# Trace of a batched product: A held whole per batch in two buffers, the next A loaded between the current B row tiles, B worked row tile by row tile, the last B tiles loaded in column pieces

## The chip, the cores and the metric

The kernel runs on one core of one Trainium2 chip. Times are device microseconds of that core. "Time" is the time of a whole execution, given as the median of several; "span" is the time from the first to the last instruction in the one profiled execution of a kernel, and it is about 1.7 us shorter than the time. All positions in time ("at 693.7 us") count from the start of the span.

## The reference, cut to what matters

```python
def setup_inputs():
    B, N = 8, 2176
    return {"a": randn(B, N, N) as float32, "b": randn(B, N, N) as float32}

def reference(a, b):
    prod = np.matmul(a, b)
    return np.diagonal(prod, axis1=1, axis2=2).sum(axis=-1)    # 8 numbers
```

The trace of A·B is the sum of A[i,k]·B[k,i] over all i and k. No matrix product is needed: each element of A meets one element of the transposed B once. The inputs are 303 MB, and every byte is used once.

## The kernel before

2176 is 17 blocks of 128. A and B arrive as row tiles of 128 x 2176 elements; the load casts them from float32 to bfloat16, so 544 KB are written for each (the page has 303.04 MB read and 151.54 MB written by the loads). TensorE transposes 128 x 128 blocks of B into PSUM (the memory of the kernel's `psum` tiles), and VectorE multiplies each such strip with the matching part of A and sums it into one column of `acc` (one custom product instruction, CUSTOM_DVE_ANT_0, and one short one that by its name reads the accumulator; the page has 680 of each, 602 and 82 ns in the mean). B is worked in groups of four row tiles: for each column block j, the four blocks of the group are transposed side by side, which gives products of 512 columns. The fifth group has one tile, and products of 128 columns.

```python
    KGW = 4                                            # B row tiles in a group
    a_pool = ctx.enter_context(tc.tile_pool(name="a_pool", bufs=2 * NT))     # 34 tiles, two batches
    b_pool = ctx.enter_context(tc.tile_pool(name="b_pool", bufs=2 * KGW))    # 8 tiles
    ...
    for bi in range(BATCH):
        for j_blk in range(NT):
            a_tile = a_pool.tile([P, N], dt, tag="a")
            nc.gpsimd.dma_start(out=a_tile, in_=a[bi, j_blk * P:(j_blk + 1) * P, :])
        for kg in range(N_KG):                         # 4, 4, 4, 4, 1 tiles
            for kc in range(kc_lo, kc_hi):
                b_tile = b_pool.tile([P, N], dt, tag="b")
                nc.gpsimd.dma_start(out=b_tile, in_=b[bi, kc * P:(kc + 1) * P, :])
            for j_blk in range(NT):
                psum_tile = psum_pool.tile([P, F], dt, tag="bT")
                for i, b_tile in enumerate(b_chunks):
                    nc.tensor.transpose(psum_tile[:, i * P:(i + 1) * P],
                                        b_tile[:, j_blk * P:(j_blk + 1) * P], identity)
                nc.vector.tensor_tensor_reduce(out=scratch[:, :fw],
                    in0=a_tiles[j_blk][:, kc_lo * P:kc_hi * P], in1=psum_tile[:, :fw],
                    ..., accum_out=acc[:, ...])
        # ... sum of acc into one column per batch
    # ... after the last batch: matmul with ones over the partitions, copy, store of 8 numbers
```

At most eight loads are in flight: in both traces no load issue starts before the load eight issues ahead of it has landed (0.28 us after it at the earliest, 0.53 us in the median). I take that for a limit of the framework that schedules the program.

Of the kernel before, what the change touches and what calls it, by code (L numbers as in the profile page):

```python
# [1 line left out]

# [6 lines left out]


@with_exitstack
def kernel(
    ctx: ExitStack,
    tc: tile.TileContext,
    a: bass.AP,
    b: bass.AP,
    out: bass.AP,
):
    nc = tc.nc  # L20
    P = 128
    BATCH, N, N2 = a.shape
    assert N == N2
    assert N % P == 0
    NT = N // P

    KGW = 4
    F = KGW * P
    N_KG = (NT + KGW - 1) // KGW

    dt = mybir.dt.bfloat16

    const = ctx.enter_context(tc.tile_pool(name="const", bufs=1))
    identity = const.tile([P, P], dt, tag="identity")
    make_identity(nc, identity)
    ones = const.tile([P, 1], mybir.dt.float32, tag="ones")
    nc.vector.memset(ones, 1.0)  # L37
    batch_accs = const.tile([P, BATCH], mybir.dt.float32, tag="batch_accs")
    result_tile = const.tile([P, BATCH], mybir.dt.float32, tag="result")

    a_pool = ctx.enter_context(tc.tile_pool(name="a_pool", bufs=2 * NT))
    b_pool = ctx.enter_context(tc.tile_pool(name="b_pool", bufs=2 * KGW))
    psum_pool = ctx.enter_context(tc.tile_pool(name="psum", bufs=7, space=bass.MemoryType.PSUM))
    psum_small = ctx.enter_context(tc.tile_pool(name="psum_small", bufs=1, space=bass.MemoryType.PSUM))
    scratch_pool = ctx.enter_context(tc.tile_pool(name="scratch", bufs=4))
    acc_pool = ctx.enter_context(tc.tile_pool(name="acc", bufs=2))

    for bi in range(BATCH):
        a_tiles = []
        for j_blk in range(NT):  # L50
            a_tile = a_pool.tile([P, N], dt, tag="a")
            nc.gpsimd.dma_start(out=a_tile, in_=a[bi, j_blk * P:(j_blk + 1) * P, :])  # L52
            a_tiles.append(a_tile)

        acc = acc_pool.tile([P, NT * N_KG], mybir.dt.float32, tag="acc")

        for kg in range(N_KG):
            kc_lo = kg * KGW
            kc_hi = min(kc_lo + KGW, NT)
            gw = kc_hi - kc_lo  # L60
            fw = gw * P

            b_chunks = []
            for kc in range(kc_lo, kc_hi):
                b_tile = b_pool.tile([P, N], dt, tag="b")
                nc.gpsimd.dma_start(out=b_tile, in_=b[bi, kc * P:(kc + 1) * P, :])  # L66
                b_chunks.append(b_tile)

            for j_blk in range(NT):
                psum_tile = psum_pool.tile([P, F], dt, tag="bT")  # L70
                for i, b_tile in enumerate(b_chunks):
                    nc.tensor.transpose(  # L72
                        psum_tile[:, i * P:(i + 1) * P],
                        b_tile[:, j_blk * P:(j_blk + 1) * P],
                        identity,
                    )
                scratch = scratch_pool.tile([P, F], dt, tag="scr")
                nc.vector.tensor_tensor_reduce(  # L78
                    out=scratch[:, :fw],
                    in0=a_tiles[j_blk][:, kc_lo * P:kc_hi * P],  # L80
                    in1=psum_tile[:, :fw],
                    scale=1.0,
                    scalar=0.0,
                    op0=mybir.AluOpType.mult,
                    op1=mybir.AluOpType.add,
                    accum_out=acc[:, j_blk * N_KG + kg: j_blk * N_KG + kg + 1],
                )

        nc.vector.reduce_sum(  # L89
            out=batch_accs[:, bi:bi + 1], in_=acc, axis=mybir.AxisListType.X  # L90
        )

    batch_psum = psum_small.tile([1, BATCH], mybir.dt.float32, tag="bp")
    nc.tensor.matmul(batch_psum, ones, batch_accs, start=True, stop=True)  # L94
    nc.vector.tensor_copy(out=result_tile[:1, :BATCH], in_=batch_psum)  # L95

    nc.sync.dma_start(
        out=out.rearrange("(a b) -> a b", a=1),
        in_=result_tile[:1, :BATCH],
    )  # L100


# [1 line left out]
_INS = ['a', 'b']  # L104
_OUTS = [((8,), 'float32')]


# [23 lines left out]
```

## Time and profile before

| | before |
|---|---|
| time, median of 3 | 737.29 us (737.23 to 737.42) |
| span | 735.6 us |
| full DMA rate | 213 to 215 GB/s written, twice that read |
| last load landed (landing records) | 721.2 us |
| last product to end of span | 2.7 us |

The lines below are from the page of the kernel before: the span, the busy time of each engine with its share, one row of the picture in 40 slices of 18.4 us (GB/s is what the core's 16 DMA engines wrote), and two of the DMA queues with packets, MB and their share of the 16 engines' span.

```profile
span 735.6 us, 7232 instructions
...
PE 271.7 (37%) x2314; PEld 217.7 (30%) x2314; DVE 364.8 (50%) x1370; POOL 144.4 (20%) x278
...
GB/s 175 213 214 215 213 215 213 214 214 214 214 213 214 214 214 214 213 214 213 214 214 213 214 213 214 214 213 215 213 214 214 213 214 214 214 214 213 161 209 29
...
q8 instruction: 18, 0.29, 0.1%
q14 instruction: 20, 0.16, 0.1%
```

No compute engine is near its limit: VectorE (DVE) is busy half the time. The GB/s row stands at 213 to 215 from the second slice to slice 37. Two slices stand out: 161 in slice 38, and 29 in the last. The two queues that the page marks "instruction" I read, by that name, as fetches of the program itself: 18 of 16 KB on q8 and 20 of 8 KB on q14 in the DMA records.

The next lines are stretches of time: busy time and count for each engine, the granted TensorE clock, the DMA share and GB/s.

```profile
core 0: us, PE busy (x) PEld busy (x) DVE busy (x) POOL busy (x), PEclk, DMA share, GB/s
...
690.00:697.00 7.00, 4.24 (x28) 2.74 (x26) 7.00 (x25) 2.11 (x4) 0.50 0.47 83
697.00:710.00 13.00, 8.40 (x86) 7.42 (x87) 12.30 (x41) 2.12 (x4) 0.76 1.05 212
710.00:715.00 5.00, 4.78 (x50) 4.58 (x48) 5.00 (x17) 0.00 (x0) 0.62 1.06 214
715.00:720.00 5.00, 1.94 (x19) 1.57 (x17) 4.94 (x17) 0.53 (x1) 0.72 0.95 178
```

Between 690 and 697 us the DMA writes 83 GB/s in place of 214. The timeline of GpSimd (POOL), which issues the loads, says why; the columns are start, duration, engine, line, operation, and in brackets how long the engine was idle before and what ended that.

```profile
676.64 0.53 POOL L66 DMA_DIRECT2D b_tile<-in_b_dram  x1 [2.12 <-DMA a_tile<-in_a_dram]
693.69 2.11 POOL L66 DMA_DIRECT2D b_tile<-in_b_dram  x4 [16.52 <-PE psum_tile L72]
704.09 2.12 POOL L66 DMA_DIRECT2D b_tile<-in_b_dram  x4 [8.29 <-PE psum_tile L72]
```

In the last batch no A loads are left to issue between the B loads, so GpSimd waits 16.52 us until TensorE has used up a group of B tiles and frees their buffers. After that comes the end of the kernel, here in the timeline of VectorE:

```profile
719.56 0.68 DVE L78 CUSTOM_DVE_ANT_0 scratch<-a_tile,psum_tile 128x512 bf16<-128x512 bf16 x1
...
720.17 0.68 DVE L78 CUSTOM_DVE_ANT_0 scratch<-a_tile,psum_tile 128x512 bf16<-128x512 bf16 x1
...
729.30 0.28 DVE L78 CUSTOM_DVE_ANT_0 scratch<-a_tile,psum_tile 128x128 bf16<-128x128 bf16 x1
...
729.51 0.28 DVE L78 CUSTOM_DVE_ANT_0 scratch<-a_tile,psum_tile 128x128 bf16<-128x128 bf16 x1
...
732.63 0.28 DVE L78 CUSTOM_DVE_ANT_0 scratch<-a_tile,psum_tile 128x128 bf16<-128x128 bf16 x1
...
732.96 0.24 DVE L89 TENSOR_REDUCE batch_accs<-acc 128x1 f32<-128x85 f32 x1
733.49 0.15 DVE L95 COPY result_tile<-batch_psum 1x8 f32<-1x8 f32 x1 [0.29 <-PE batch_psum L94]
```

Products of 512 columns follow each other every 0.61 us, those of 128 columns every 0.205 us. The last load has landed at 721.2 us, but VectorE has the rest of the fourth group and all of the fifth still before it, until 732.9 us; then come the sum of the batch, the matmul with ones, the copy and the store.

The trace also records 16 completions for each load (4354 in all: 16 for each of 272 loads, and 2), which I read as one for each of the core's 16 DMA engines. These records are not in a view of the profile; numbers called "landing records" in this text were worked out from them: the landing of a load is the last of its 16 completions, and its spread is the time from the first to the last. For the 11th load the spread is 0.78 us; for the 255th of 272 it is 7.38 us, and of these the last completion alone is 4.46 us behind the 15th. The records don't name the engine; I read the last completion as that of one engine that falls behind the others by more and more, called the slowest engine here. TensorE's first transpose of a B tile, where it waits for nothing else, starts 0.04 us after the last of the 16 completions.

### The profile page before, as it was taken

Reading aid. Unit: us, or ns where it says so; the run is one execution under the profiler, and the core shown is the slowest. Engines: PE = TensorE matmul, PEld = TensorE weight load, DVE = VectorE, ACT = ScalarE, POOL = GpSimd, SP = SyncE. Lnnn points to the kernel's source line nnn. Section 1 sums busy time; section 2 is a strip of 40 time slices with the busy share of each in tenths; the row PEclk is TensorE's granted clock in tenths of the full one; section 3 lists DMA queues with packets and bytes.
Section 4 is the critical chain, followed back from the end, with each engine's and each line's share of the span. In section 5 each row is a group of like instructions: output and inputs, shape, how many; then the busy total and the mean of one; then the engine's idle time right before and its main releaser. Section 6 shows DMA issues by size and latency. Waiting matters only on the chain.

```text
span 735.6 us, 7232 instructions
## 1 busy us (share of the span) xinstructions
PE 271.7 (37%) x2314; PEld 217.7 (30%) x2314; DVE 364.8 (50%) x1370; POOL 144.4 (20%) x278
## 2 busy tenths in 40 slices
PE   0016441174412744035450453505453054520665
PEld 0005430163301533024340343403342034410454
DVE  0007673087610967019570285704766056750698
POOL 4221221112121221212222122221222222221110
PEclk9999775557655556556655556555556556665575
DMA  8999999999999999999999999999999999999891
GB/s 175 213 214 215 213 215 213 214 214 214 214 213 214 214 214 214 213 214 213 214 214 213 214 213 214 214 213 215 213 214 214 213 214 214 214 214 213 161 209 29
DMA packets 39208, 152.00 MB, mean 207 GB/s; under 512 B 4354, under 2 KB 4354, under 8 KB 39170
## 3 DMA queue, kind: packets, MB, share of 16 engines
q0 software_dynamic: 39168, 151.54, 102.2%
q8 instruction: 18, 0.29, 0.1%
q14 instruction: 20, 0.16, 0.1%
q1 hardware_dynamic: 2, 0.00, 0.0%
HBM read 303.04 MB, written 0.00 MB: 412 GB/s over the span
## 4 chain that ended last, share of the span: by engine, by line
DMA 80%; issue 16%; POOL 1%; DVE 1%; PE 0%; POOLq 0%; DVEq 0%
DMA b_tile<-in_b_dram 51%; DMA a_tile<-in_a_dram 29%; POOL b_tile L66 1%; DVE scratch L78 1%; DVE acc L78 1%; POOL a_tile L52 0%; PE psum_tile L72 0%; POOLq L66 0%; POOL identity masks.py:199 0%; DVE batch_accs L89 0%; PE batch_psum L94 0%; DVEq L78 0%; POOL identity masks.py:197 0%; DVE result_tile L95 0%; POOLq masks.py:199 0%
## 5 line engine op out<-in xcount | busy, mean ns | idle before, releaser
L78 DVE CUSTOM_DVE_ANT_0 scratch<-a_tile,psum_tile 128x512 bf16<-128x512 bf16 (+1 forms) x680 | 362.3, 602 | 367.4 <-PE psum_tile L72 367.2
L72 PE MATMUL psum_tile<-identity,b_tile 128*128 128x128 bf16 x2312 | 271.5, 286 | 460.3 <-DMA b_tile<-in_b_dram 434.1
L72 PEld LDWEIGHTS <-b_tile 128*128 128x128 bf16 x2312 | 217.6, 132 | 513.8 <-DMA b_tile<-in_b_dram 465.6
L66 POOL DMA_DIRECT2D b_tile<-in_b_dram x136 | 71.8, 532 | 332.6 <-PE psum_tile L72 180.2
L52 POOL DMA_DIRECT2D a_tile<-in_a_dram x136 | 72.2, 533 | 238.0 <-DMA b_tile<-in_b_dram 112.4
L78 DVE DVE_READ_ACCUMULATOR2_ANT acc<- 128x1 f32 x680 | 55.9, 82 | 0.0
L89 DVE TENSOR_REDUCE batch_accs<-acc 128x1 f32<-128x85 f32 x8 | 1.9, 241 | 0.3
L94 PE MATMUL batch_psum<-batch_accs,ones 128*1 128x8 f32 x2 | 0.2, 173 | 1.5 <-DVE batch_accs L89 1.5
L94 PEld LDWEIGHTS batch_psum<-batch_accs,ones 128*1 128x1 f32 x2 | 0.1, 80 | 1.8 <-DVE batch_accs L89 1.8
L37 DVE MEMSET ones<- 128x1 f32 x1 | 0.1, 59 | 0.8 <-PEq L115 0.8
masks.py:199 POOL TENSOR_SCALAR_AFFINE_SELECT identity<-identity 128x128 bf16<-128x128 bf16 x1 | 0.3, 305 | 0.1
L95 DVE COPY result_tile<-batch_psum 1x8 f32<-1x8 f32 x1 | 0.2, 155 | 0.3 <-PE batch_psum L94 0.3
masks.py:197 POOL MEMSET identity<- 128x128 bf16 x1 | 0.2, 204 | 0.3 <-POOLq L115 0.3
L115 POOL MEMSET const-float32-0.0<- 128x1 f32 x1 | 0.1, 98 | 0.2 <-issue 0.2
L115 POOL MEMSET const-bfloat16-1.0<- 128x1 bf16 x1 | 0.1, 101 | 0.0
L115 POOL MEMSET const-uint8-127<- 128x1 uint8 x1 | 0.1, 101 | 0.0
L115 POOL MEMSET const-float32-1.0<- 128x1 f32 x1 | 0.1, 98 | 0.0
## 6 DMA issues: line engine op xcount, KB each, us to landing
a_tile<-in_a_dram POOLq DMA_DIRECT2D x136, 544.0 KB, 20.6
b_tile<-in_b_dram POOLq DMA_DIRECT2D x136, 544.0 KB, 20.3
out_dram<-result_tile SPq DMA_DIRECT2D x1, 0.0 KB
```

Of the source, the lines that this page charges most:

```text
L37: nc.vector.memset(ones, 1.0)
L52: nc.gpsimd.dma_start(out=a_tile, in_=a[bi, j_blk * P:(j_blk + 1) * P, :])
L66: nc.gpsimd.dma_start(out=b_tile, in_=b[bi, kc * P:(kc + 1) * P, :])
L72: nc.tensor.transpose(psum_tile[:, i * P:(i + 1) * P], b_tile[:, j_blk * P:(j_blk + 1) * P], identity,)
L78: nc.vector.tensor_tensor_reduce(out=scratch[:, :fw], in0=a_tiles[j_blk][:, kc_lo * P:kc_hi * P], in1=psum_tile[:, :fw], scale=1.0, scalar ...
L89: nc.vector.reduce_sum(out=batch_accs[:, bi:bi + 1], in_=acc, axis=mybir.AxisListType.X)
L94: nc.tensor.matmul(batch_psum, ones, batch_accs, start=True, stop=True)
L95: nc.vector.tensor_copy(out=result_tile[:1, :BATCH], in_=batch_psum)
L115: nc = _bacc.Bacc("TRN2", target_bir_lowering=False, num_devices=1)
```

## The change

Its intent: hold the whole A of a batch as one tile, so that one product can span several row tiles of A; then each B row tile can be worked off by itself as soon as it lands, with products of 768, 768 and 640 columns, and no group of four has to be complete first. The next A is loaded between the B tiles, so that GpSimd has something to issue. The last two B tiles come in four column pieces, so that work on them can start before they are complete.

```diff
-    a_pool = ctx.enter_context(tc.tile_pool(name="a_pool", bufs=2 * NT))
-    b_pool = ctx.enter_context(tc.tile_pool(name="b_pool", bufs=2 * KGW))
+    CHUNKS = [(0, 6), (6, 12), (12, NT)]
+    LAST_CHUNKS = [(0, 6), (6, 12), (12, 16), (16, NT)]
+    a_pool = ctx.enter_context(tc.tile_pool(name="a_pool", bufs=2))      # tiles [P, NT, N]
+    b_pool = ctx.enter_context(tc.tile_pool(name="b_pool", bufs=10))     # tiles [P, ROWS, N]
+    a_next = a_pool.tile([P, NT, N], dt, tag="a")
+    for gi in range(len(groups)):
+        load_a(a_next, 0, gi)                        # all 17 row tiles of the first A
     ...
+    for bi in range(BATCH):
+        a_all = a_next
+        last = bi == BATCH - 1
+        if not last:
+            a_next = a_pool.tile([P, NT, N], dt, tag="a")
+        for gi, (start, m) in enumerate(b_groups):   # ROWS = 1: m is 1, 17 tiles
+            b_tile = b_pool.tile([P, ROWS, N], dt, tag="b")
+            pieces = last and gi >= len(b_groups) - 2
+            chunks = LAST_CHUNKS if pieces else CHUNKS
+            if pieces:
+                for lo, hi in chunks:
+                    nc.gpsimd.dma_start(out=b_tile[:, 0, lo * P:hi * P],
+                                        in_=b[bi, start:start + P, lo * P:hi * P])
+            else:
+                load(b_tile[:, 0:m, :], b[bi], start, m)
+            if not last:
+                load_a(a_next, bi + 1, gi)
+            for lo, hi in chunks:
+                ...
+                psum_tile = psum_pool.tile([P, 6, P], dt, tag="bT")
+                for u in range(lo, hi):
+                    nc.tensor.transpose(psum_tile[:, u - lo, :], b_tile[...], identity)
+                nc.vector.tensor_tensor_reduce(out=scratch[:, :w, :],
+                    in0=a_all[:, lo:hi, start + s:...], in1=psum_tile[:, :w, :],
+                    ..., accum_out=acc[:, col:col + 1])
```

More of the change, by code (lines that the diff above doesn't have):

```diff
@@ L5, with row_groups @@
 import concourse.tile as tile
-from concourse import bass_utils, mybir
-from concourse import bass_isa
+from concourse import mybir
 from concourse.masks import make_identity
 from concourse._compat import with_exitstack
+def row_groups(n, p, rows):
+    groups, at = [], 0
+    while at < n:
+        m = min(rows, (n - at) // p)
+        groups.append((at, m))
+        at += m * p
+    return groups
 @with_exitstack
@@ L22 @@
     BATCH, N, N2 = a.shape
-    assert N == N2
-    assert N % P == 0
+    assert N == N2 and N % P == 0
     NT = N // P
-    KGW = 4
-    F = KGW * P
-    N_KG = (NT + KGW - 1) // KGW
+    ROWS = 1
+    CHUNKS = [(0, 6), (6, 12), (12, NT)]
+    LAST_CHUNKS = [(0, 6), (6, 12), (12, 16), (16, NT)]
     dt = mybir.dt.bfloat16
+    f32 = mybir.dt.float32
     const = ctx.enter_context(tc.tile_pool(name="const", bufs=1))
+    a_pool = ctx.enter_context(tc.tile_pool(name="a_pool", bufs=2))
+    b_pool = ctx.enter_context(tc.tile_pool(name="b_pool", bufs=10))
@@ new lines, with load @@
+    psum_pool = ctx.enter_context(tc.tile_pool(name="psum", bufs=7, space=bass.MemoryType.PSUM))
+    psum_small = ctx.enter_context(tc.tile_pool(name="psum_small", bufs=1, space=bass.MemoryType.PSUM))
+    scratch_pool = ctx.enter_context(tc.tile_pool(name="scratch", bufs=2))
+    acc_pool = ctx.enter_context(tc.tile_pool(name="acc", bufs=2))
+    groups = row_groups(N, P, ROWS)
+    slot_cols = [(start + r, m) for start, m in groups for r in range(m)]
+    def load(dst, src, start, m):
+        rows = src[start:start + P * m, :].rearrange("(p r) k -> p r k", r=m)
+        nc.gpsimd.dma_start(out=dst, in_=rows)
@@ L34, with load_a @@
+    def load_a(a_all, bi, gi):
+        start, m = groups[gi]
+        slot = start // P
+        load(a_all[:, slot:slot + m, :], a[bi], start, m)
+    a_next = a_pool.tile([P, NT, N], dt, tag="a")
+    for gi in range(len(groups)):
+        load_a(a_next, 0, gi)
     identity = const.tile([P, P], dt, tag="identity")
     make_identity(nc, identity)
-    ones = const.tile([P, 1], mybir.dt.float32, tag="ones")
+    ones = const.tile([P, 1], f32, tag="ones")
     nc.vector.memset(ones, 1.0)
-    batch_accs = const.tile([P, BATCH], mybir.dt.float32, tag="batch_accs")
@@ L39 @@
-    result_tile = const.tile([P, BATCH], mybir.dt.float32, tag="result")
-    a_pool = ctx.enter_context(tc.tile_pool(name="a_pool", bufs=2 * NT))
-    b_pool = ctx.enter_context(tc.tile_pool(name="b_pool", bufs=2 * KGW))
-    psum_pool = ctx.enter_context(tc.tile_pool(name="psum", bufs=7, space=bass.MemoryType.PSUM))
-    psum_small = ctx.enter_context(tc.tile_pool(name="psum_small", bufs=1, space=bass.MemoryType.PSUM))
-    scratch_pool = ctx.enter_context(tc.tile_pool(name="scratch", bufs=4))
@@ L46 @@
-    acc_pool = ctx.enter_context(tc.tile_pool(name="acc", bufs=2))
-    for bi in range(BATCH):
-        a_tiles = []
-        for j_blk in range(NT):
-            a_tile = a_pool.tile([P, N], dt, tag="a")
-            nc.gpsimd.dma_start(out=a_tile, in_=a[bi, j_blk * P:(j_blk + 1) * P, :])
-            a_tiles.append(a_tile)
-        acc = acc_pool.tile([P, NT * N_KG], mybir.dt.float32, tag="acc")
-        for kg in range(N_KG):
-            kc_lo = kg * KGW
-            kc_hi = min(kc_lo + KGW, NT)
-            gw = kc_hi - kc_lo
-            fw = gw * P
-            b_chunks = []
-            for kc in range(kc_lo, kc_hi):
-                b_tile = b_pool.tile([P, N], dt, tag="b")
-                nc.gpsimd.dma_start(out=b_tile, in_=b[bi, kc * P:(kc + 1) * P, :])
-                b_chunks.append(b_tile)
-            for j_blk in range(NT):
-                psum_tile = psum_pool.tile([P, F], dt, tag="bT")
-                for i, b_tile in enumerate(b_chunks):
-                    nc.tensor.transpose(
-                        psum_tile[:, i * P:(i + 1) * P],
-                        b_tile[:, j_blk * P:(j_blk + 1) * P],
-                        identity,
-                    )
-                scratch = scratch_pool.tile([P, F], dt, tag="scr")
-                nc.vector.tensor_tensor_reduce(
-                    out=scratch[:, :fw],
-                    in0=a_tiles[j_blk][:, kc_lo * P:kc_hi * P],
-                    in1=psum_tile[:, :fw],
-                    scale=1.0,
-                    scalar=0.0,
-                    op0=mybir.AluOpType.mult,
-                    op1=mybir.AluOpType.add,
-                    accum_out=acc[:, j_blk * N_KG + kg: j_blk * N_KG + kg + 1],
-                )
@@ new lines @@
+    batch_accs = const.tile([P, BATCH], f32, tag="batch_accs")
+    result_tile = const.tile([P, BATCH], f32, tag="result")
+    for bi in range(BATCH):
+        a_all = a_next
+        last = bi == BATCH - 1
+        b_groups = row_groups(N, P, 1 if last else ROWS)
+        acc = acc_pool.tile([P, NT * len(LAST_CHUNKS)], f32, tag="acc")
+        col = 0
+        if not last:
[6 more added lines that the diff above has]
+                for lo, hi in chunks:
+                    nc.gpsimd.dma_start(
+                        out=b_tile[:, 0, lo * P:hi * P],
+                        in_=b[bi, start:start + P, lo * P:hi * P],
+                    )
+            else:
[3 more added lines that the diff above has]
+            for lo, hi in chunks:
+                for s in range(m):
+                    w = hi - lo
+                    psum_tile = psum_pool.tile([P, 6, P], dt, tag="bT")
+                    for u in range(lo, hi):
+                        c0, step = slot_cols[u]
+                        nc.tensor.transpose(
+                            psum_tile[:, u - lo, :],
+                            b_tile[:, s, c0:c0 + step * (P - 1) + 1:step],
+                            identity,
+                        )
+                    scratch = scratch_pool.tile([P, 6, P], dt, tag="scr")
+                    nc.vector.tensor_tensor_reduce(
+                        out=scratch[:, :w, :],
+                        in0=a_all[:, lo:hi, start + s:start + s + m * (P - 1) + 1:m],
+                        in1=psum_tile[:, :w, :],
+                        scale=1.0,
+                        scalar=0.0,
+                        op0=mybir.AluOpType.mult,
+                        op1=mybir.AluOpType.add,
+                        accum_out=acc[:, col:col + 1],
+                    )
+                    col += 1
@@ L89 @@
         nc.vector.reduce_sum(
-            out=batch_accs[:, bi:bi + 1], in_=acc, axis=mybir.AxisListType.X
+            out=batch_accs[:, bi:bi + 1], in_=acc[:, :col], axis=mybir.AxisListType.X
         )
-    batch_psum = psum_small.tile([1, BATCH], mybir.dt.float32, tag="bp")
+    batch_psum = psum_small.tile([1, BATCH], f32, tag="bp")
     nc.tensor.matmul(batch_psum, ones, batch_accs, start=True, stop=True)
```

## The prediction

> **What bounds the kernel now.** The DMA. The page's slices show 213 to 215 GB/s written (bf16; twice that, 428 GB/s, read as fp32) from the second slice to slice 37, while VectorE is busy 50% and TensorE 37%. [...] The change moves the same bytes. Only head, gaps and tail can be won.
>
> - Head: first load issued at 1.28 us, full rate from 4 us: 3.3 us lost.
> - Gap: in the last batch GpSimd waits 16.5 us (timeline, to 693.7 us) for TensorE to free B buffers; windows 690 to 697 us show 59 and 116 GB/s. That looks like 5 us lost. It is not: in the trace's landing records the 16 DMA engines of one load end up to 7.4 us apart by then (0.8 us at the start), and the slowest engine idles only 0.6 us here. A load has landed when all 16 have ended[...]. The last load lands at 721.4 us.
> - Tail: from there to 735.6 us, 14.2 us: VectorE works off products of 512 columns at 0.61 us and 17 of 128 at 0.205 us (chain of waits), then 2.7 us of sum, matmul, copy, store.
>
> **The change, costed.**
> 1. Products become 768/768/640 columns: by the two spacings 1.046 ns a column plus 0.074 us, 2.50 us a B tile (estimate), against 5.2 us of loads in batches 0 to 6 and 2.605 us in the last, B-only batch. VectorE barely keeps up there; TensorE needs 17 x 0.104 = 1.8 us.
> 2. Tail: a B tile is finished about 0.8 us (first six transposes) plus 2.5 us after landing. As VectorE is nearly as slow as the loads, the pieces can't shorten that much: the whole tile before them leaves VectorE behind. Last product 3.1 us after the last landing, then 2.7 us: tail 5.8 instead of 14.2 us, gain 8.4 us, all on the critical path.
> 3. The 16.5 us stall goes: 0.6 us. The A loads start before the identity: 0.3 us.
> 4. Pieces: 6 more DMAs, some with 256-byte rows: cost 0.4 us (guess).
> 5. New stall: the first load into the next A waits until VectorE has read the A of the batch before. Three B loads are issued ahead of it, so about 7 us of loads stay queued: no starvation at the 6 boundaries.
> 6. The slowest engine's lag grows about 0.55 us at two places per batch where GpSimd stalls. The new order keeps one; if the stalls are the cause, up to 3.5 us are won. I count 1.5.
>
> Sum: span 735.6 - 8.4 - 0.9 + 0.4 - 1.5 = 725.2; with the 1.7 us between span and metric, about 726.5 us.
>
> **Predicted: 726.5 us, 721.5 to 731.** Chances: faster by over 2% 0.13, within 2% 0.85, slower 0.02.
>
> **Right, if:** DMA at 214 GB/s to the last slice; last landing at 717 to 722 us; tail after the last B landing under 7 us; long GpSimd stalls once per batch. **Wrong, if:** dips at batch boundaries (step 5), VectorE backlog growing through the last batch (step 1), a tail near 2 us (step 2).
>
> **What would make it wrong.** The lag vanishing altogether (near 722), starvation at boundaries, or the three-dimensional product slower than 1.05 ns a column.

The loads are issued about 2.605 us apart, and they land 2.608 us (before) and 2.607 us (after) apart in the median; 272 times 2.605 us is 708.6 us. That they can't go faster was my assumption, and no run tests it. That a load has landed when all 16 have ended rests here on the 0.04 us above.

Some of its other figures beside what the traces show. For the 0.6 us that the slowest engine idles: the four landings after the one at 697.0 us, the last at 708.1 us, take 0.68 us more than four steps of 2.605 us, with a q14 fetch at 701.5 us among them. A transpose, put at 0.104 us, starts 0.107 us after the one before it in the most frequent spacing of both traces. The 0.8 us from the landing to the first product are 0.91 us in the trace after, where VectorE waits for it. The 0.4 us of step 4 was a guess; e2 gives 0.3 us for it. What the 256-byte rows (256 such packets in the DMA records) have to do with that was not tested.

## The result, and the profile after

| | before | after |
|---|---|---|
| time, median of 4 | 737.26 us | 726.33 us (726.15 to 726.47) |
| span | 735.6 us | 724.6 us |
| last load landed (landing records) | 721.2 us | 718.8 us |
| spread of the 255th load (landing records) | 7.4 us | 5.0 us |
| last landing to end of span | 14.4 us | 5.8 us |
| VectorE instructions | 1370 | 830 |

The ratio of the times is 0.9851 (95% interval 0.9837 to 0.9865): 1.5% faster, clear of noise, but within the 2% that counts as the same. A ratio here is not quite the ratio of the medians.

The same lines of the page, after:

```profile
span 724.6 us, 6370 instructions
...
PE 263.7 (36%) x2314; PEld 228.9 (32%) x2314; DVE 352.1 (49%) x830; POOL 147.6 (20%) x284
...
GB/s 176 214 213 214 213 214 214 213 214 213 215 212 214 213 215 213 214 214 213 214 213 215 213 214 213 214 214 214 213 213 214 213 214 214 213 214 213 214 213 93
...
q8 instruction: 18, 0.29, 0.1%
q14 instruction: 13, 0.11, 0.0%
```

The GB/s row now stays at 212 to 215 from the second slice to slice 39. The q14 row went from 20 instruction fetches to 13. The same stretches of time (columns as before):

```profile
690.00:697.00 7.00, 4.00 (x47) 3.39 (x45) 6.77 (x15) 1.44 (x3) 0.80 1.05 212
697.00:710.00 13.00, 8.06 (x85) 7.02 (x85) 12.14 (x31) 2.63 (x5) 0.73 1.06 211
710.00:715.00 5.00, 3.67 (x33) 3.41 (x34) 4.96 (x11) 1.05 (x2) 0.50 1.02 170
715.00:720.00 5.00, 3.48 (x37) 2.81 (x35) 5.00 (x15) 0.00 (x0) 0.82 0.14 20
```

The dip at 690 to 697 us is gone (212 GB/s). But look at 715 to 720 us: 20 GB/s at a DMA share of 0.14, about two engines of 16. Of the 16 completions of the last load 13 are in by 715.7 us; the other three come at 716.8, 717.3 and 718.8 us, and the last is its landing. The waits of GpSimd (engine, line, what for: us in total, times, longest) show the new wait of the change:

```profile
POOL a_next L54 <- DVE batch_accs L121: 78.7, 6, 13.2
```

Six times, once for each batch boundary, GpSimd waits up to 13.2 us until VectorE has finished with the A that the next load will overwrite. And the end of the kernel on VectorE:

```profile
714.18 0.95 DVE L109 CUSTOM_DVE_ANT_0 scratch<-a_next,psum_tile 128x768 bf16<-128x768 bf16 x1
...
715.06 0.95 DVE L109 CUSTOM_DVE_ANT_0 scratch<-a_next,psum_tile 128x768 bf16<-128x768 bf16 x1
...
715.94 0.82 DVE L109 CUSTOM_DVE_ANT_0 scratch<-a_next,psum_tile 128x640 bf16<-128x640 bf16 x1
...
716.68 0.95 DVE L109 CUSTOM_DVE_ANT_0 scratch<-a_next,psum_tile 128x768 bf16<-128x768 bf16 x1
...
721.63 0.28 DVE L109 CUSTOM_DVE_ANT_0 scratch<-a_next,psum_tile 128x128 bf16<-128x128 bf16 x1
...
721.95 0.21 DVE L121 TENSOR_REDUCE batch_accs<-acc 128x1 f32<-128x53 f32 x1
722.45 0.15 DVE L127 COPY result_tile<-batch_psum 1x8 f32<-1x8 f32 x1 [0.29 <-PE batch_psum L126]
```

The 768-column products follow each other every 0.88 us, and VectorE has no gap from 711.6 us to the last product at 721.6 us; then 2.7 us of sum, matmul, copy and store, as before. So the 11.0 us of span came from two places: 8.6 us from the work after the last landing, and 2.4 us from an earlier last landing.

### The profile page after: what moved, and what is told of

It reads as the page before. It is cut to its first block, busy times and chain, and to the rows that moved or that the text cites. A ratio compares the mean times of both kernels' runs of the same rounds, so it can differ in the third digit from the quotient of the medians.

```text
span 724.6 us, 6370 instructions
## 1 busy us (share of the span) xinstructions
PE 263.7 (36%) x2314; PEld 228.9 (32%) x2314; DVE 352.1 (49%) x830; POOL 147.6 (20%) x284
## 4 chain that ended last, share of the span: by engine, by line
DMA 90%; issue 6%; POOL 2%; DVE 1%; PE 1%; POOLq 0%; ACTq 0%
DMA b_tile<-in_b_dram 76%; DMA a_next<-in_a_dram 14%; POOL a_next L54 2%; PE psum_tile L103 1%; DVE scratch L109 1%; DVE acc L109 0%; DVE batch_accs L121 0%; POOL b_tile L54 0%; POOLq L54 0%; POOL identity masks.py:197 0%; PE batch_psum L126 0%; DVE result_tile L127 0%; POOLq masks.py:199 0%; ACTq L158 0%
## 5 line engine op out<-in xcount | busy, mean ns | idle before, releaser
L109 DVE CUSTOM_DVE_ANT_0 scratch<-a_next,psum_tile 128x768 bf16<-128x768 bf16 (+1 forms) x410 | 349.2, 903 | 369.1 <-PE psum_tile L103 366.5
L103 PE MATMUL psum_tile<-identity,b_tile 128*128 128x128 bf16 x2312 | 263.5, 306 | 455.6 <-DMA b_tile<-in_b_dram 452.3
L103 PEld LDWEIGHTS <-b_tile 128*128 128x128 bf16 x2312 | 228.8, 143 | 490.1 <-DMA b_tile<-in_b_dram 490.1
L54 POOL DMA_DIRECT2D b_tile<-in_b_dram x134 | 71.2, 531 | 281.2 <-DMA b_tile<-in_b_dram 228.4
L54 POOL DMA_DIRECT2D a_next<-in_a_dram x136 | 72.2, 534 | 268.0 <-DMA a_next<-in_a_dram 180.3
L109 DVE DVE_READ_ACCUMULATOR2_ANT acc<- 128x1 f32 x410 | 33.8, 83 | 0.0
L87 POOL DMA_DIRECT2D b_tile<-in_b_dram x8 | 4.2, 527 | 16.9 <-DMA b_tile<-in_b_dram 16.9
L121 DVE TENSOR_REDUCE batch_accs<-acc 128x1 f32<-128x51 f32 (+1 forms) x8 | 1.6, 206 | 0.3
```

Of the source, the lines that this page charges most:

```text
L54: nc.gpsimd.dma_start(out=dst, in_=rows)
L87: nc.gpsimd.dma_start(out=b_tile[:, 0, lo * P:hi * P], in_=b[bi, start:start + P, lo * P:hi * P],)
L103: nc.tensor.transpose(psum_tile[:, u - lo, :], b_tile[:, s, c0:c0 + step * (P - 1) + 1:step], identity,)
L109: nc.vector.tensor_tensor_reduce(out=scratch[:, :w, :], in0=a_all[:, lo:hi, start + s:start + s + m * (P - 1) + 1:m], in1=psum_tile[:, :w, :],
L121: nc.vector.reduce_sum(out=batch_accs[:, bi:bi + 1], in_=acc[:, :col], axis=mybir.AxisListType.X)
```

## The experiments

The theories to be told apart were these. For the tail: working the last batch row tile by row tile gives the 8.6 us, and the pieces and the interleaved loads give nothing; the rivals credit the pieces or the order of the loads. For the last landing: it is set by the slowest DMA engine alone. Why that engine lags had two rival explanations. My prediction suspected the stalls of GpSimd. Comparing the landing records with the DMA records of the two traces gave another: the lag grows in steps, and each step follows an 8 KB instruction fetch on queue q14. This is the comparison, worked out from those records (times in us; "landing" is the first late landing after the fetch, "step" is how much more than 2.605 us it came after the landing before it; a step of 0.8 or more gives 0.3 to 0.5 back at the next load, so that about 0.5 stays of each):

```
before  fetch  199.6  252.9  289.3  342.6  379.0  432.7  468.7  522.1  558.5  611.8  648.2  701.5
        landing 201.4  254.4  291.1  344.1  380.9  434.1  470.6  523.6  560.3  613.3  650.0  703.0
        step    0.49   0.84   0.51   0.81   0.51   1.06   0.51   0.83   0.51   0.81   0.51   0.82
after   fetch  229.6  302.1  371.4  444.0  508.8  588.5  660.4  706.9
        landing 232.4  303.6  374.3  445.5  510.9  590.0  663.2  708.4
        step    0.51   0.83   0.55   0.83   0.53   0.81   0.51   0.83
```

From 195 us on to the last landing, three q14 fetches before (283.8, 453.0 and 621.8 us) and two after (333.5, 554.2) have no such step. The traces say whose they are likely to be. They come at about the 198th, 327th and 455th instruction of GpSimd, those of its sequencer counted, so some 128 apart; the fetches with a step come 121 to 137 instructions of VectorE apart. No run tested the fetches of GpSimd. Before 195 us the pattern does not hold: the q14 fetches at 163.9 us before and 150.5 us after show no step, while late landings at 107.5 us before and at 120.0 and 161.7 us after come 2.0 to 2.1 us after a fetch on q8, which carries 16 KB at a time.

The changed kernel has 540 VectorE instructions fewer. If their fetches cause the lag, then the number of VectorE instructions moves the last landing, although VectorE, busy for 303 of the first 667 us after, is not the limit in batches 0 to 6.

In the runs, on three chips, the kernel before was timed again each time, at medians of 737.44 to 737.53 us (737.26 us beside the changed kernel). The changed kernel was not timed again with them, so differences of 0.3 us between it and a run are no more than that scatter. Landings come from one profile of each run.

### e1: the dip removed from the kernel before

```diff
-    b_pool = ctx.enter_context(tc.tile_pool(name="b_pool", bufs=2 * KGW))
+    b_pool = ctx.enter_context(tc.tile_pool(name="b_pool", bufs=3 * KGW))
```

> The kernel before with 12 B buffers in place of 8, nothing else of it edited; the dip to 59 and 116 GB/s at 690 to 697 us should vanish. Theory 'slowest DMA engine': the last landing (721.4 us) is set by the slowest of the 16 DMA engines, which idled only about 0.6 us in the dip, so the time falls by 0.3 to 1.0 us, to about 736.5 us. Rival 'mean rate': the dip costs what the mean rate lost, so the time falls by about 5 us, to about 732 us.

Measured: 737.17 us against 737.53 us of the kernel before, ratio 0.9997 (0.9984 to 1.0009). The edit has a side effect that I had not written down: with more buffers, the scheduler also issues all B loads of a batch ahead of the next A. The stretches (columns as before):

```profile
690.00:697.00 7.00, 4.32 (x29) 2.74 (x26) 7.00 (x25) 1.59 (x3) 0.50 1.05 211
...
710.00:715.00 5.00, 4.66 (x49) 4.30 (x47) 5.00 (x17) 0.00 (x0) 0.67 0.88 177
715.00:720.00 5.00, 2.04 (x18) 1.73 (x18) 4.98 (x17) 0.00 (x0) 0.68 0.09 18
```

The dip is gone: 211 GB/s from 690 to 697 us. Nearly nothing was gained: 0.36 us between the medians, which the interval doesn't tell from nothing. The rate falls 5 us earlier instead, and from 715 to 720 us it is 18 GB/s at a share of 0.09: that is the work of between one and two engines of 16. The last load lands at 721.00 us, 0.2 us earlier than before; the first of its 16 engines had finished at 713.0 us. In the kernel before, the 16 completions of the last load lie 1.4 us apart (719.8 to 721.2 us), here 8.0 us: the dip had only brought the others back to the slowest engine, and had cost next to no time. The "mean rate" reading, 5 us, is refuted; the prediction's 0.6 us was above the 0.2 to 0.4 us that were measured. The side effect makes e1 a test of the stalls theory too: the order of the loads is another and the longest wait of GpSimd is 6.3 us in place of 16.5 us, but VectorE's instructions are the same, and so are the 20 fetches on q14 and the spread of the 255th load (7.5 us, before 7.4 us).

### e2: no column pieces

```diff
-            pieces = last and gi >= len(b_groups) - 2
+            pieces = False
```

> The changed kernel without the column pieces (last two B tiles whole). Theory of the prediction: VectorE needs 2.5 us a tile and the loads 2.6 us, so the whole tile before the pieces leaves it behind and the pieces buy nothing: 726.3 us, at most 0.5 us either way; last landing about 0.3 us earlier. Rival: the pieces shorten the tail by most of one tile's VectorE time, so without them 728 to 728.5 us.

Measured: 726.24 us, against 726.33 us with the pieces; last landing 718.4 us in place of 718.8 us. The pieces buy nothing and cost 0.3 us at the landing, most of which the tail gives back (5.8 us in place of 6.0 us).

### e3 and e4: more, narrower products in batches 0 to 6

```diff
-            chunks = LAST_CHUNKS if pieces else CHUNKS
+            chunks = LAST_CHUNKS if pieces else CHUNKS if last else NARROW
# e3: NARROW = [(0, 4), (4, 8), (8, 12), (12, 16), (16, NT)]
# e4: NARROW = [(i, i + 1) for i in range(NT)]
# both: acc gets as many columns as there are products
```

> The changed kernel with products of 4 columns blocks (5 per B tile instead of 3) in batches 0 to 6, last batch as it is. VectorE instructions go from 832 to about 1310, near the 1372 of before; VectorE still needs only 2.65 us of 5.2 us a tile, and GpSimd's stalls stay as they are. Theory 'instruction fetch' (each 8 KB fetch of 128 VectorE instructions delays the slowest DMA engine by about 0.52 us): 3.7 more fetches, the last landing 1.5 to 2.3 us later, about 728.3 us. Rival 'stalls' (the prediction's step 6: the lag comes from GpSimd stalls): 726.3 us, unchanged.

> The changed kernel with 17 products of one column block per B tile in batches 0 to 6, last batch as it is: about 4160 VectorE instructions, 26 more fetches of 8 KB; VectorE 17 x 0.21 = 3.5 us of 5.2 us a tile, so not the limit. Theory 'instruction fetch': 26 x 0.52 = 13.5 us later, about 740 us. Rival 'stalls': 726.3 us.

Measured: e3 728.77 us, e4 747.09 us (ratio 1.0131 against the kernel before, slower than it clear of noise, though within 2%). The page of e3, span and instruction queues:

```profile
span 727.3 us, 7091 instructions
...
q14 instruction: 19, 0.16, 0.1%
```

and of e4:

```profile
span 745.4 us, 11335 instructions
...
q8 instruction: 18, 0.29, 0.1%
q14 instruction: 52, 0.43, 0.1%
```

In e3 the order of the loads is the one of the changed kernel, GpSimd waits for VectorE as there (six times, up to 13.1 us), and VectorE has time left (an estimated 2.65 us of 5.2 us a tile, from the product spacings), so the stalls theory, which expected 726.3 us, has fallen. e4 is less clean: GpSimd waits there 92 times for TensorE to free a B buffer, up to 4.9 us, and the DMA rate falls to 197 to 212 GB/s in most slices of the last third, so that part of its time may have another cause. The q14 fetches went from 13 to 19 and to 52, while q8, with 18 fetches, stays as the number of TensorE instructions does. The last landing moved from 718.78 us to 721.85 us in e3, 3.07 us for 6 fetches, and to 740.33 us in e4, 21.55 us for 39 fetches: 0.51 and 0.55 us a fetch. The size of a fetch's delay was as expected; their number was not. I had expected 128 instructions to a fetch (121 to 137 lie between the fetches with a step in the two traces), and by the page's count it is about 80 (476 more instructions and 6 fetches in e3, 3332 and 39 in e4), so both runs came out slower than I had said. My count was at fault, not the 128: the page leaves out what VectorE's sequencer runs, mostly waits for semaphores (453 of them in the changed kernel). With these the traces hold 1286 VectorE instructions in the changed kernel, 2007 in e3 and 6251 in e4, which is 120 and 127 more for each further fetch. In e4 the spread of the 255th load was 15.4 us.

e3 is also an undo of this part of the change: with 1306 VectorE instructions, close to the 1370 of before, the changed kernel loses 2.4 us in the median (2.8 us in the profiled execution: 3.1 us at the landing, of which 0.3 us come back in the tail, 5.5 us in place of 5.8 us; why, I did not pursue).

### e5: fewer, wider products in batches 0 to 6

```diff
-    psum_pool = ... (name="psum", bufs=7, ...)             # tiles [P, 6, P]
+    psum_pool = ... (name="psum", bufs=2, ...)
-            chunks = LAST_CHUNKS if pieces else CHUNKS
+            chunks = LAST_CHUNKS if pieces else CHUNKS if last else [(0, NT)]
+            psum_whole = psum_pool.tile([P, 24, P], dt, tag="bT")   # one per B tile
             for lo, hi in chunks:
-                    psum_tile = psum_pool.tile([P, 6, P], dt, tag="bT")
+                    psum_tile = psum_whole[:, lo:hi, :]
```

> The changed kernel with one product of 2176 columns per B tile in batches 0 to 6[...], last batch and its pieces as they are: 356 VectorE instruction rows in place of 832. Theory 'instruction fetch' (0.52 us a fetch on the slowest DMA engine, and by the runs so far one fetch per 80 or so VectorE instructions): about 6 fetches fewer, 3.1 us, but the second slowest engine is only 2.0 us ahead of the slowest at the end, so the last landing is about 2 us earlier: 724.0 to 724.6 us. Rival: the lag has another cause tied to the order of the loads, 726.3 us.

Measured: 754.24 us, slower than both kernels; my expectation of the time was wrong. The landing was as expected, though: the last load landed at 716.81 us, 2.0 us earlier than in the changed kernel, and the spread of the 255th load fell to 2.5 us. The loss is in the last batch, on VectorE:

```profile
692.50 0.08 DVE L110 DVE_READ_ACCUMULATOR2_ANT acc<- 128x1 f32 x1
...
694.35 0.95 DVE L110 CUSTOM_DVE_ANT_0 scratch<-a_next,psum_whole 128x768 bf16<-128x768 bf16 x1 [0.89 <-PE psum_whole L104]
...
696.10 0.82 DVE L110 CUSTOM_DVE_ANT_0 scratch<-a_next,psum_whole 128x640 bf16<-128x640 bf16 x1 [0.78 <-PE psum_whole L104]
696.84 0.08 DVE L110 DVE_READ_ACCUMULATOR2_ANT acc<- 128x1 f32 x1
```

One B tile takes 4.34 us (692.50 to 696.84 us) where a load lands every 2.6 us, and two of its three products wait 0.8 to 0.9 us for TensorE. In my build, all chunks of a B tile shared one PSUM tile, and inside it TensorE's transposes of a chunk did not run ahead of VectorE's product of the chunk before. The scheduler's dependence on the whole tile is my reading of it; that the shared tile was at fault is shown by e9, which gives the last batch its own small tiles again.

### e6: all B tiles of the last batch in pieces

```diff
-            pieces = last and gi >= len(b_groups) - 2
-            chunks = LAST_CHUNKS if pieces else CHUNKS
+            pieces = last
+            chunks = LAST_CHUNKS if last and gi >= len(b_groups) - 2 else CHUNKS
```

> The changed kernel with every B tile of the last batch loaded in column pieces (768, 768, 640 columns; the last two as they are). If pieces were useless only because the whole tile ahead of them leaves VectorE behind, then here VectorE never falls behind and the last product ends about 1.7 us after the last landing in place of 2.9 us; the 30 more DMAs cost about 0.1 us each 2, 1.5 to 2.3 us in all, so the time is 726 to 727.5 us. Rival: VectorE is behind for another reason, the tail stays 2.9 us and the time is 728 us or more.

Measured: 726.63 us. The last load landed at 720.23 us, 1.45 us later than in the changed kernel, and from there to the end of the span it took 4.7 us in place of 5.8 us. So pieces do shorten the tail once VectorE is not already behind, as the theory says, by 1.1 us; the 30 more DMAs cost a little more than that, 0.05 us each at the landing. The expectation's 0.1 us for two was an estimate; e2's 0.3 us for six are as much.

### e7: groups of four again, in the last batch only

```diff
+        per = 4 if last else 1
+        for g0 in range(0, len(b_groups), per):
+            held = []
+            ... load the per tiles of the group into held ...
+            for chunk in CHUNKS:
+                for b_tile, start, m in held[::-1]:
+                    col = work(b_tile, [chunk], start, m, col)
```

> The changed kernel, no pieces, whose last batch is worked in groups of four B tiles again, the last landed of a group first, so that VectorE starts on a group only when all four have landed. All else (whole A, interleaved loads, wide products) is as in the changed kernel. Theory 'tail by row tiles': the last product ends 10 to 11 us after the last landing in place of 2.9 us: 733.5 to 734.5 us. Rival: the gain came from the new order of the loads and the missing stalls, 726 to 728 us.

Measured: 733.90 us, 7.7 us slower than e2, which has no pieces either. The last load landed at 718.44 us, exactly when it does in e2. The timeline of VectorE:

```profile
717.04 0.95 DVE L94 CUSTOM_DVE_ANT_0 scratch<-a_next,psum_tile 128x768 bf16<-128x768 bf16 x1 [1.20 <-PE psum_tile L88]
...
728.76 0.08 DVE L94 DVE_READ_ACCUMULATOR2_ANT acc<- 128x1 f32 x1
...
729.62 0.21 DVE L121 TENSOR_REDUCE batch_accs<-acc 128x1 f32<-128x51 f32 x1
```

VectorE is idle for 1.20 us before the fourth group and then runs without a gap from 717.04 us to 729.6 us, 11.1 us past the last landing. Everything else of the change was still in place, so working row tile by row tile in the last batch is what gives the tail's gain, 7.7 us of the 8.6 us (the tail is 13.8 us here and 6.0 us in e2); the interleaved loads and the missing stalls do not. For the rest, e2 gives the pieces 0.2 us; what gives the last 0.6 to 0.7 us was not tested.

### e8: next A loaded after the B tiles, not between them

```diff
-            if not last:
-                load_a(a_next, bi + 1, gi)
             ...
+        if not last:
+            for gi in range(len(groups)):
+                load_a(a_next, bi + 1, gi)
```

> The changed kernel with the loads of the next A issued after all B tiles of the current batch, not between them. Theory: the DMA is full either way and the last batch is the same, 725.8 to 726.9 us. Rival 'interleaving keeps the DMA full': VectorE needs 2.5 us of 2.6 us a tile in each B phase, falls behind, B buffers come free late, the DMA starves at the end of each batch, over 729 us.

Measured: 726.19 us, the same as the changed kernel (726.33 us). The interleaving buys nothing: with the loads in either order the last landing is the same within 0.05 us (below). This run takes the long waits away that the change had brought: the longest wait of GpSimd is 4.7 us in place of 13.2 us. The lag did not follow: there are 13 fetches on q14 as in the changed kernel, the spread of the 255th load is 4.7 us (5.0 us there), and the last load lands at 718.73 us (718.78 us there). With e1 and e3 that is a third run against the stalls as the cause.

### e9 and e10: the wide products, built properly

The seven batches with one product of 2176 columns per B tile use a PSUM pool of two tiles of 24 blocks; before the last batch that pool is closed and one of seven tiles of 6 blocks is opened.

```diff
+    wide = ExitStack()
+    psum_pool = wide.enter_context(tc.tile_pool(name="psum", bufs=2, space=bass.MemoryType.PSUM))
     for bi in range(BATCH):
+        if last:
+            wide.close()
+            psum_pool = ctx.enter_context(tc.tile_pool(name="psum_last", bufs=7, space=bass.MemoryType.PSUM))
+        blocks = 6 if last else 24
-            pieces = last and gi >= len(b_groups) - 2
-            chunks = LAST_CHUNKS if pieces else CHUNKS
+            pieces = False                        # e10: pieces = last, loads of (0, 12), (12, NT)
+            chunks = CHUNKS if last else [(0, NT)]
-                    psum_tile = psum_pool.tile([P, 6, P], dt, tag="bT")
+                    psum_tile = psum_pool.tile([P, blocks, P], dt, tag="bT")
```

> As e5_wide17 in batches 0 to 6 (one product of 2176 columns per B tile), but the last batch gets its own PSUM tiles[...] so that TensorE and VectorE overlap there as in the changed kernel; no column pieces. Theory 'instruction fetch': last landing about 2 us earlier than in the changed kernel, same tail of about 5.7 us, 724.0 to 724.7 us. If the slowness of e5_wide17 came from the wide products and not from its shared PSUM tile in the last batch, over 726.3 us.

> As e9_wide_narrow_last, with every B tile of the last batch loaded in two column pieces (1536 and 640 columns). The 17 more DMAs should cost 0.6 to 1.0 us (e6_all_pieces: 30 more cost 1.45 us at the last landing), and VectorE, no longer behind, should end 2.0 to 2.3 us after the last landing in place of 2.9 us: 723.9 to 724.8 us, within 0.4 us of e9_wide_narrow_last.

Measured: e9 724.75 us (724.69 to 724.91, 5 runs), ratio 0.9828 against the kernel before; e10 724.91 us (724.86 to 725.03, 4 runs). The page of e9:

```profile
span 722.9 us, 5616 instructions
...
q14 instruction: 7, 0.06, 0.0%
```

There are 7 fetches on q14 in place of 13, the spread of the 255th load is 2.7 us in place of 5.0 us, and the last load lands at 717.15 us. The nearest comparison is with e2, which has no pieces either and differs only in the products and PSUM tiles of batches 0 to 6: 1.3 us earlier, 1.5 us of time. That is less than 6 fetches at 0.5 us, 3.1 us. I put that down to the slowest engine no longer standing alone: in e9 the second slowest engine ended the 255th load 0.2 us before the slowest, in the changed kernel 2.4 us before it. What holds up the slowest engine of e9 looks like the q8 fetches, whose number stays: after 195 us nine landings come 0.3 to 1.0 us late, each 2.0 to 2.4 us after a 16 KB fetch on q8 and none after one on q14. No run changed the number of TensorE's instructions, so this is read off and not tested. e9 beats the changed kernel by 1.6 us, and the kernel before by 1.7%, still within 2%. e10 shows again that pieces pay for themselves at most: its last landing is 0.4 us later than in e9, its tail 0.2 us shorter. Part of my expectation failed here: the last product should have ended 2.0 to 2.3 us after the last landing, and it ended 3.0 us after it; I did not pursue why.

## Why the prediction was right

The time was predicted as 726.5 us, and it is 726.33 us. So close a hit is partly luck. The terms add up to a span of 725.2 us and, with the 1.7 us, to 726.9 us; "about 726.5" was written 0.4 us too low, towards the result. And the sum was better than its terms, so here they are one by one.

- **The bound.** Right, and so were the signs named in advance: the last landing at 718.8 us (717 to 722 was said), a tail under 7 us, one long GpSimd wait per batch. Both kernels run at 214 GB/s for all but the head, the tail and the dip of the kernel before, and the DMA's time for the bytes didn't move. That the 428 GB/s read (214 GB/s written) can't be exceeded was my assumption; no slice of the two pages is above 215 GB/s written, and no run tests it.
- **Step 1, product widths.** Right: the three products of a tile were predicted at 0.88, 0.88 and 0.74 us and take that (715.06 - 714.18, 715.94 - 715.06 and 716.68 - 715.94 us in the timeline after). VectorE keeps up in the last batch with almost nothing to spare: it has a gap of 0.55 us at 709 us and none after 711.6 us.
- **Step 2, the tail.** Right: 5.8 us as predicted, a gain of 8.6 us where 8.4 us was predicted. e7 shows that row tiles in the last batch give 7.7 us of it, and e2 that the pieces give 0.2 us at most.
- **Step 3, the 16.5 us stall.** The mechanism is right, the size is too high: 0.6 us predicted, 0.2 us at the landing and 0.36 us in time by e1, neither clear of noise. The 0.3 us counted with it for the earlier A loads are not shown by any run (see the sum below). That this stall is not worth the 5 us that the mean rate suggests was the main trap of this profile.
- **Step 4, the pieces' cost.** Right, although guessed: 0.4 us, and 0.3 us by e2.
- **Step 5, the new wait.** Right: it is there six times, up to 13.2 us long, and the GB/s row shows nothing of it.
- **Step 6, the lag of the slowest engine.** The cause was wrong, and the size too low. I put the lag down to GpSimd's stalls, and counted 1.5 us. The lag does shrink, by 2.4 us in the spread of the 255th load, but because the wider products need fewer VectorE instructions and so fewer instruction fetches. e3 keeps the new order of the loads, puts the instructions back, and loses the gain; e1 and e8 change the order and the stalls, keep the instructions, and the lag stays. So a gain too large in step 3 and ones too small here and in step 2 partly cancelled each other, and the range was wide enough for the wrong cause.

The tail and the landing add up: 8.6 us from the one, 7.7 us of it shown by e7, and 2.4 us from the other. The table of fetches has 12 steps before and 8 after, at about 0.52 us each 2.1 us; the missing dip gives 0.2 us by e1; the pieces take 0.3 us away by e2. That is 2.0 us of the 2.4 us. The 17th landing comes 0.4 us sooner (48.7 and 48.3 us), but runs with the new head have it anywhere from 48.3 to 48.5 us, and e1 with the old head at 48.5 us, so that the head gives the rest is not shown. The fetches' price per piece, the dip and the pieces were tested by runs of their own. That the fetches delay one DMA engine is a reading of the last completion, which stands alone; why one, and which, can't be read from these traces: the landing records don't name the engine.

## What to carry to other kernels

When a kernel runs at full DMA rate, a dip in the mean rate need not cost its area: here 83 in place of 214 GB/s over 7 us, about 4 us at full rate, was worth 0.36 us in the medians, not clear of noise (e1). TensorE began 0.04 us after the last of a load's 16 completions, and these were 7.4 us apart, so look at how far apart they end before pricing a gap. What is left to win is the work after the last landing, and here it was set by how many loads had to be complete before work on them could start (7.7 us, e7); a finer last load helped only where the compute engine was not already behind when it arrived (1.1 us off the tail in e6, against 0.2 us off it in the changed kernel, by e2). And an instruction can cost more than its busy time: in this DMA-bound kernel, fewer and wider instructions on an engine with time to spare still moved the end, by 0.51 us (e3) to 0.55 us (e4) for each fetch of 8 KB, and by less in e9, where the two slowest engines ended 0.2 us apart and 6 fetches fewer gave 1.3 us. A fetch came for every 120 (e3) to 127 (e4) further VectorE instructions with those of its sequencer, about 80 of those that the page counts.
